# Tokens stored normed but unmodulated, scale and shift applied to transposed tokens, and one projection pass as a single fp32 product

## The chip, the cores and the metric

The kernel runs on one core of one Trainium2 chip, in fp32, as one launch. The metric is the device time of a run in microseconds; the median of three runs counts. Times in the profile are those of one further, profiled execution.

## The reference

Two transformer blocks over T = 512 tokens of width D = 1024. Each ends with a mixture of experts. What matters here is the end of the mixing, the modulated norm ahead of the router, and the experts:

```python
# block 1
mix = concat([attn, hg], -1) @ w_out
x = x + ga1 * rmsnorm(mix, ln1_post)
h = rmsnorm(x, ln2_pre) * (1.0 + sc2) + sh2
y = hierarchical_moe(h, ...)            # 32 experts, 2 per token, width 256
x = x + ga2 * rmsnorm(y, ln2_post)

# block 2
h = modulate(norm(x), shift, scale)     # h * (1 + scale) + shift
out = moe_ffn(h, ...)                   # 64 experts, 8 per token, and a shared one

def hierarchical_moe(h, ...):
    ...
    xs = tok[order // TOP_K]            # rows of h, by expert
    hg = ragged_dot(xs, w_gate, sizes)
    hu = ragged_dot(xs, w_up, sizes)
    ys = ragged_dot(silu(hg) * hu, w_down, sizes)
```

`sc2`, `sh2` (and their namesakes in block 2) are vectors over the features, the same for all tokens, from a product of the condition `c` with `w_ada`.

## The kernel before, in words

**Stages.** One program runs head, dense1 (projection in, windowed attention, a gated recurrence, projection out), the first experts, dense2, out2 (the second block's output projection, its router and its shared expert), the second experts and a last norm. Every instruction is issued through a recording helper at line 131, so every row of the profile names L131 and groups are told apart by tiles. Names: `w` and `wx` are chunks of weights (512 KB each, in two pools of buffers), `hi` and `lo` their split, `u` a 128x1024 row tile, `h` a 128x512 one, `bank` a PSUM bank, `xg` gathered token rows, `xT` their transposes, `a` and `aT` the hidden layer and its transposes, `ha_d` and `hb_d` the stored rows of the two blocks in HBM.

**Order of the work.** A cooperative scheduler (`Flow`, 152) runs generators and lets each go on when a model of the engines' times says so; the order on each engine follows from it. SP issues all weight chunks in one list, in order, as buffers come free.

**Dense products** (`steps`, 397). Each chunk of weights is split by ACT (`split_hi`, 344: a copy rounded to fp32r) and DVE (`split_lo`, 359: the rest), and `mm3` (460) adds three fp32r products, hi x lo, hi x hi and lo x hi. The left operand, the tokens, is split in the same way by `mixed` (1036). The output projection of dense1 (823 to 849) makes two passes p = 0, 1 over the 8 chunks of `w_out`, one for the token tiles 0 and 1, one for 2 and 3; each chunk gives four 128x512 products. A chunk marked `raw` is not split; the experts' chunks are of this kind, and theirs are single fp32 products.

**Post.pair** (1814) takes a pass's four banks: mean square on ACT, gate and residual on DVE, the sum to HBM (SP), the norm into two `u` tiles. `Route.tile` (1903) transposes each on PE and applies scale and shift per feature while copying out of PSUM (ACT the first four slices, DVE the last four), multiplies by the router's weights and lets DVE pick. When PE has taken the rows (`seen`), Post.pair has POOL multiply the normed rows by the scale and add the shift, both held as 128x1024 row broadcasts, and store them to `ha_d` or `hb_d` by POOL's own DMA queue. `Post.load` makes the three row broadcasts (gate, shift, scale).

**Routing.** `choose` picks the first experts after two token tiles, `finish` orders all after the fourth. `queue` (2164) lets SP load only the first experts' weights after `choose`, the rest after `finish`.

**Experts** (`run`, 2373). Per block of up to 128 tokens: a gather of rows by POOL's indirect DMA into `xg` (2218), 8 transposes on PE and two copies out of PSUM, one on ACT and one on DVE (`xT`, 2244), gate and up products over 4 chunks (`gu`, 2276), SiLU and product (`act`, 2284), transposes of `a` (2305), the down product over 2 chunks (`dn`, 2321) and a scatter-add (2330). The first stage has 32 blocks, the second 71. A block over 96 tokens makes four 128x512 products in `dn`, two per chunk.

Of the kernel before, what the change touches and what calls it, by code (L numbers as in the profile page):

```python
# [21 lines left out]
P = 128  # L22
# [191 lines left out]
class Body:  # L214
# [182 lines left out]
    def steps(self, queued, n, jobs, evac, kd=KD, pre=None, early=None):  # L397
# [6 lines left out]
        def one(c, j, sel):  # L404
            ahead = None
            for i in sel:
# [3 lines left out]
                for jj in range(c.kd):  # L410
                    s = slice(jj * n + c0, jj * n + c0 + width)
                    wt = (c.hl[0][:, s], c.hl[1][:, s])
                    ac = act(j + jj)
                    L, R = (wt, ac) if kind == "T" else (ac, wt)
                    self.mm3(outs[i], L, R, j + jj == 0, j + jj == kd - 1)
                    if jj < c.kd - 1:
                        yield
# [8 lines left out]
            self.split_lo(ahead)  # L426

# [103 lines left out]
    def ada_mask(self):  # L531

        nc = self.nc
        m = self.mask = self.c_const([P, 256])
# [34 lines left out]
    def ada_row(self, acc, b, part, dst, gain=None, plus=0.0, cols_=None):  # L569
# [11 lines left out]
        nc.sync.dma_start(cols(dst), r)  # L581
# [90 lines left out]
    def dense1(self, x1_d, h2_d, route, x1, acc1, acc2):  # L672
# [9 lines left out]
        for p in range(2):  # L682
            q_["o", p] = self.add_chunks(I["w_out"], D, KD)
        x1.queue(route)
# [28 lines left out]
        post = Post(self, True, mod[0:3], I["x"], x1_d, h2_d, route)  # L713
        route.mod = self.c_tile([P, 8]), self.c_tile([P, 8])
# [3 lines left out]
        def row(i):  # L718
            yield 8.0
            post.load(i, self.u)  # L720

        def ada(parts):
            for part in parts:
# [3 lines left out]
                if part < 5:  # L727
                    rows.append(fl.start(row(part - 2)))
# [98 lines left out]
        for p in range(2):  # L827
            fl.until_(lambda: E.done[2 * p] and E.done[2 * p + 1] and E.att[2 * p] and E.att[2 * p + 1])
            jobs = []
            for t in (2 * p, 2 * p + 1):  # L830
                act = (lambda t: lambda j: tuple(x[:, j % 4 * P : j % 4 * P + P] for x in E.half[t][j // 4]))(t)
                jobs += [("tok", half * 512, 512, act, full) for half in range(2)]
# [203 lines left out]
    def mixed(self, E, n, half, x, done):  # L1036

        hl = self.h(F32R), self.h(F32R)
# [143 lines left out]
    def dense2(self, acc_d, x2_d, route):  # L1182
# [15 lines left out]
        route.mod = self.c_tile([P, 8]), self.c_tile([P, 8])  # L1198
# [255 lines left out]
    def out2(self, mg, t_mg, x2_d, x3_d, h2_d, route, acc_d, e2):  # L1454
# [4 lines left out]
        post = Post(self, False, m[2:5], x2_d, x3_d, h2_d, route)  # L1459
        for i in range(3):  # L1460
            post.load(i, self.r4)
# [333 lines left out]
class Post:  # L1795


    def __init__(self, body, post, rows, x_d, x1_d, h2_d, route):
        self.b, self.post, self.rows, self.x_d, self.x1_d, self.h2_d = body, post, rows, x_d, x1_d, h2_d
        self.v, self.xs = [None] * 3, {}  # L1800
        self.seen, self.evac = route.seen, [False] * 2

    def load(self, i, vec):
        self.v[i] = vec()
        self.b.bcast(self.v[i], self.rows[i])
# [8 lines left out]
    def pair(self, p, outs, then):  # L1814
        b, nc = self.b, self.b.nc
        gate, shift, scale = self.v
# [24 lines left out]
        for i in range(2):  # L1841
            if i:
                nc.scalar.activation(ms[i], xs[i], AF.Copy, scale=r[:, i : i + 1])
            else:
                nc.vector.tensor_scalar(out=ms[i], in0=xs[i], scalar1=r[:, i : i + 1], scalar2=None, op0=ALU.mult)
            ts.append(b.flow.start(then(2 * p + i, ms[i]), MARGIN2))
        yield 1
        yield from b.wait_(lambda: self.seen >= {2 * p, 2 * p + 1})
        for i in range(2):
            nc.gpsimd.tensor_tensor(out=ms[i], in0=ms[i], in1=scale, op=ALU.mult)  # L1850
            nc.gpsimd.tensor_tensor(out=ms[i], in0=ms[i], in1=shift, op=ALU.add)
            nc.gpsimd.dma_start(self.h2_d[(2 * p + i) * P : (2 * p + i + 1) * P], ms[i])
# [3 lines left out]
class Route:  # L1856
# [6 lines left out]
    def __init__(self, body, E, plan, first, chosen, router, name):  # L1863
# [6 lines left out]
        self.sels, self.parts, self.chosen, self.seen = [], [None] * NT, False, set()  # L1870
# [32 lines left out]
    def tile(self, t, h, keep=None):  # L1903
# [7 lines left out]
        self.seen.add(t)  # L1911
# [245 lines left out]
class Experts:  # L2157
# [86 lines left out]
    def xT(self, x):  # L2244
        b, C = self.b, x.C
        x.xT = self.xTs[x.n % len(self.xTs)]
        for half in range(2):
# [3 lines left out]
            sl = slice(half * 4, half * 4 + 4)  # L2251
            if half:
                b.nc.vector.tensor_copy(x.xT[:, sl, :C], pt[:, :, :C])
            else:
                b.nc.scalar.activation(x.xT[:, sl, :C], pt[:, :, :C], AF.Copy)
# [227 lines left out]
def cols(w, n0, n):  # L2483

    return w[:, n0 : n0 + n].reshape(P, KD * n)
# [111 lines left out]
```

## Time and profile before

| what | value |
|---|---|
| median of 3 runs | 2090.17 us (2090.0 to 2093.3) |
| profiled execution | 2091.46 us, span 2089.7 us |
| PE, DVE, ACT, POOL busy | 87%, 51%, 27%, 17% of the span |
| HBM traffic | 495.48 MB read, 60.53 MB written, 266 GB/s over the span |
| POOL TENSOR_TENSOR of 128x1024 | 16, 40.3 us busy |
| DVE `lo`, 105 of them | 135.9 us busy |
| ACT `hi`, 105 of them | 108.8 us busy |
| ACT copies to `xT`, 103 of them | 40.0 us busy |

The time of a run lies 1.8 us above the span from the first to the last instruction. Shares are means over stages of different kinds, so they say little about any one of them: a stage is read by a window of its own. In a timeline, the number in brackets behind a row is how long its engine stood idle before it, and what released it. A weight load of PE (PEld) and its matmul (PE) are separate rows.

### The profile page before, as it was taken

How to read it: one execution, taken by the hardware profiler on the slowest of the kernel's cores; microseconds unless marked ns; L12 is line 12 of the kernel's file. 1: busy time of each engine (PE TensorE's matmuls, PEld its weight loads, DVE VectorE, ACT ScalarE, POOL GpSimd, SP SyncE). 2: the span in 40 equal slices, each digit the busy share in tenths (PEclk: the TensorE clock that was granted, in tenths of full speed). 3: DMA queues.
4: the chain of work that ended last, by engine and by line, in shares of the span. 5: the costliest groups of instructions: out<-in, count | busy, mean ns of one | idle time of the engine just before them, and what ended most of it. 6: DMA issues, size and time to landing. Idle time of an engine off the chain costs nothing. (4 is left out here: it accounts for less than half of the span.)

```text
span 2089.7 us, 35845 instructions
## 1 busy us (share of the span) xinstructions
PE 1807.8 (87%) x13085; PEld 1175.0 (56%) x13085; DVE 1061.4 (51%) x2885; ACT 559.3 (27%) x1146; POOL 359.7 (17%) x375
## 2 busy tenths in 40 slices
PE   4999986398878579888889998779999999999993
PEld 3777765354444457667767776655544445455551
DVE  5554766533223264466655655854544444444443
ACT  3522443211111252356653223410100000001011
POOL 1000002323222100000000211413222222222221
PEclk9999987599975689999999999989999999999997
DMA  9746323399999865776423557449999999999996
GB/s 338 267 153 231 141 80 140 138 347 364 376 381 380 340 221 184 259 234 173 146 84 111 181 188 265 172 152 361 362 359 358 348 363 367 353 360 346 357 357 227
DMA packets 180167, 551.81 MB, mean 264 GB/s; under 512 B 28290, under 2 KB 40706, under 8 KB 179988
## 3 DMA queue, kind: packets, MB, share of 16 engines
q1 hardware_dynamic: 159268, 491.10, 64.1%
q0 software_dynamic: 18560, 54.88, 10.6%
q10 hardware_dynamic: 2160, 3.50, 0.5%
q8 instruction: 105, 1.72, 0.3%
q14 instruction: 74, 0.61, 0.1%
HBM read 495.48 MB, written 60.53 MB: 266 GB/s over the span
## 5 line engine op out<-in xcount | busy, mean ns | idle before, releaser
L131 PE MATMUL bank<-w,xT 128*32 128x128 f32 (+5 forms) x2988 | 312.5, 363 | 12.4 <-DMA w<-in_w_gu 11.0
L131 PE MATMUL bank<-u,hi 128*128 128x512 f32 x800 | 262.9, 411 | 9.0 <-DVE u L131 5.6
L131 POOL DMA_INDIRECT acc_d<-y,iv x103 | 148.4, 1441 | 498.6 <-DVE y L131 156.9
L131 PEld LDWEIGHTS bank<-w,xT 128*32 128x32 f32 (+5 forms) x2988 | 148.7, 128 | 130.5 <-issue 70.9
L131 PE MATMUL bank<-wx,xT 128*32 128x128 f32 (+4 forms) x1812 | 185.5, 363 | 14.7 <-DMA wx<-in_w_gu 8.8
L131 DVE TENSOR_TENSOR y<-bank,gate 32x256 f32<-32x256 f32 (+5 forms) x228 | 128.0, 561 | 109.1 <-PE bank L131 107.2
L131 PEld LDWEIGHTS bank<-u,hi 128*128 128x128 f32 x800 | 148.6, 195 | 43.6 <-DVE u L131 7.1
L131 PE MATMUL bank<-u,lo 128*128 128x512 f32 x400 | 161.6, 404 | 10.2 <-DVE lo L131 10.2
L131 ACT ACTIVATE xT<-bank 128x128 f32<-128x128 f32 (+6 forms) x103 | 40.0, 388 | 450.1 <-PE bank L131 426.8
L131 DVE TENSOR_TENSOR lo<-w,hi 128x1024 fp32r<-128x1024 f32 x105 | 135.9, 1299 | 42.9 <-ACT hi L131 39.5
L131 PE MATMUL bank<-hi,u 128*128 128x512 f32 (+1 forms) x512 | 154.5, 386 | 1.4 <-DVE u L131 1.4
L131 PEld LDWEIGHTS bank<-ident,xg 48*128 48x128 f32 (+6 forms) x824 | 99.0, 200 | 75.6 <-issue 60.3
L131 PE MATMUL bank<-w,aT 128*32 128x256 f32 (+5 forms) x664 | 126.6, 535 | 14.6 <-DMA w<-in_w_dn 10.2
L131 PEld LDWEIGHTS bank<-wx,xT 128*32 128x32 f32 (+4 forms) x1812 | 89.8, 129 | 78.9 <-issue 38.7
L131 PE MATMUL bank<-wx,aT 128*32 128x256 f32 (+5 forms) x600 | 118.9, 524 | 6.6 <-DMA wx<-in_w_dn 6.0
L131 ACT ACTIVATE hi<-w 128x1024 fp32r<-128x1024 f32 x105 | 108.8, 1049 | 48.5 <-PE bank L131 24.4
L131 PE MATMUL bank<-ident,xg 48*128 48x48 f32 (+6 forms) x824 | 112.0, 280 | 11.0 <-DMA xg<-ha_d,iv 9.5
L131 PE MATMUL bank<-lo,u 128*128 128x512 f32 (+1 forms) x256 | 105.4, 412 | 17.1 <-DVE lo L131 16.1
L131 POOL TENSOR_TENSOR u<-u,t 128x1024 f32<-128x1024 f32 x16 | 40.3, 2518 | 427.3 <-DVE u L131 352.6
L131 DVE SCALAR_TENSOR_TENSOR a<-a,iv,bank 64x256 f32<-64x256 f32 (+3 forms) x80 | 38.5, 481 | 144.1 <-ACT a L131 144.1
L131 PEld LDWEIGHTS bank<-hi,u 128*128 128x128 f32 x512 | 97.6, 196 | 19.0 <-DVE u L131 1.8
L131 ACT ACTIVATE a<-bank 64x256 f32<-64x256 f32 (+4 forms) x129 | 43.4, 337 | 238.8 <-PE bank L131 230.5
(235 smaller groups left out, 2663.5 us busy)
## 6 DMA issues: line engine op xcount, KB each, us to landing
w<-in_w_gu SPq DMA_DIRECT2D x235, 512.0 KB, 13.4
wx<-in_w_gu SPq DMA_DIRECT2D x149, 512.0 KB, 12.5
w<-in_w_dn SPq DMA_DIRECT2D x101, 512.0 KB, 13.1
wa<-in_w_ada SPq DMA_DIRECT2D x96, 512.0 KB, 6.5
wx<-in_w_dn SPq DMA_DIRECT2D x91, 512.0 KB, 13.0
w<-in_w_in SPq DMA_DIRECT2D x68, 512.0 KB, 5.6
w<-in_w_out SPq DMA_DIRECT2D x21, 512.0 KB, 7.7
nab<-in_nab SPq DMA_DIRECT2D x48, 128.0 KB, 3.9
```

Source lines behind the costliest of these rows:

```text
L131: r = f(*a, **k)
```

## The change

It does three things.

1. Post.pair stores the normed rows as they are: POOL's multiplications and additions go, and so do the row broadcasts of scale and shift, the wait for `seen`, and the stores of those two vectors to HBM. The experts' `xT` applies scale and shift instead, per feature, while copying out of PSUM, as `Route.tile` does: four operations on ACT and four on DVE per block in the place of one each. The per-feature vectors are kept to the end (`c_const`); a mask becomes bf16 to make room.
2. The 8 chunks of the second pass of the first output projection are marked raw: one fp32 product in the place of three, no `hi` and `lo`; the chunk's buffer is given back after its four products.
3. `mixed` leaves the token tiles 2 and 3 of that projection unsplit.

```diff
@@ steps (397)
-                    wt = (c.hl[0][:, s], c.hl[1][:, s])
                     ac = act(j + jj)
-                    L, R = (wt, ac) if kind == "T" else (ac, wt)
-                    self.mm3(outs[i], L, R, j + jj == 0, j + jj == kd - 1)
+                    if c.raw:
+                        self.nc.tensor.matmul(outs[i], ac, c.w[:, s], start=(j + jj == 0), stop=(j + jj == kd - 1))
+                    else:
+                        wt = (c.hl[0][:, s], c.hl[1][:, s])
+                        L, R = (wt, ac) if kind == "T" else (ac, wt)
+                        self.mm3(outs[i], L, R, j + jj == 0, j + jj == kd - 1)
...
             self.split_lo(ahead)
+            if c.raw:
+                self.used(c)
@@ ada_mask (531)
-        m = self.mask = self.c_const([P, 256])
+        m = self.mask = self.c_const([P, 256], BF16)
@@ ada_row (569)
-        nc.sync.dma_start(cols(dst), r)
+        if cols_ is None:
+            nc.sync.dma_start(cols(dst), r)
@@ dense1 (672)
         for p in range(2):
             q_["o", p] = self.add_chunks(I["w_out"], D, KD)
+        for c in q_["o", 1]:
+            c.raw = True
...
-        route.mod = self.c_tile([P, 8]), self.c_tile([P, 8])
+        route.mod = self.c_const([P, 8]), self.c_const([P, 8])
...
-                act = (lambda t: lambda j: tuple(x[:, j % 4 * P : j % 4 * P + P] for x in E.half[t][j // 4]))(t)
+                cut = lambda x, j: x[:, j % 4 * P : j % 4 * P + P]
+                act = (lambda t: lambda j: cut(E.half[t][j // 4], j) if p else tuple(cut(x, j) for x in E.half[t][j // 4]))(t)
@@ mixed (1036)
+        if n >= 2:
+            E.half[n][half] = x
+            done[n] = True
+            return
         hl = self.h(F32R), self.h(F32R)
@@ out2 (1454)
-        post = Post(self, False, m[2:5], x2_d, x3_d, h2_d, route)
-        for i in range(3):
-            post.load(i, self.r4)
+        post = Post(self, False, m[2], x2_d, x3_d, h2_d, route)
+        post.load(self.r4)
@@ Post.pair (1814)
+            nc.gpsimd.dma_start(self.h2_d[(2 * p + i) * P : (2 * p + i + 1) * P], ms[i])
             ts.append(b.flow.start(then(2 * p + i, ms[i]), MARGIN2))
-        yield 1
-        yield from b.wait_(lambda: self.seen >= {2 * p, 2 * p + 1})
-        for i in range(2):
-            nc.gpsimd.tensor_tensor(out=ms[i], in0=ms[i], in1=scale, op=ALU.mult)
-            nc.gpsimd.tensor_tensor(out=ms[i], in0=ms[i], in1=shift, op=ALU.add)
-            nc.gpsimd.dma_start(self.h2_d[(2 * p + i) * P : (2 * p + i + 1) * P], ms[i])
@@ Experts.xT (2244)
-            sl = slice(half * 4, half * 4 + 4)
-            if half:
-                b.nc.vector.tensor_copy(x.xT[:, sl, :C], pt[:, :, :C])
-            else:
-                b.nc.scalar.activation(x.xT[:, sl, :C], pt[:, :, :C], AF.Copy)
+            for k in range(4):
+                j = half * 4 + k
+                if half:
+                    b.nc.vector.tensor_scalar(out=x.xT[:, j, :C], in0=pt[:, k, :C], scalar1=A[:, j : j + 1], scalar2=B[:, j : j + 1], op0=ALU.mult, op1=ALU.add)
+                else:
+                    b.nc.scalar.activation(x.xT[:, j, :C], pt[:, k, :C], AF.Identity, scale=A[:, j : j + 1], bias=B[:, j : j + 1])
```

The order of instructions moves at three places. On PE, at the beginning of the second pass of dense1's output projection (`c_467` are the router's weights, `ctx` rows of another input that are transposed in between, DMAHW and DMASW a DMA's semaphore), before:

```order
L131 MATMUL bank<-c_467,h 128x36 [waits DVE_49] x4
L131 MATMUL bank<-ident,ctx 128x128 x2
L131 MATMUL bank<-lo,h 128x512 [waits Activation_49]
L131 MATMUL bank<-hi,h 128x512
L131 MATMUL bank<-hi,h 128x512 [waits DVE_49]
L131 MATMUL bank<-lo,h 128x512
L131 MATMUL bank<-hi,h 128x512 x2
```

and now:

```order
L131 MATMUL bank<-w,h 128x512 [waits DMAHW0_49,DVE_49,PE_49]
L131 MATMUL bank<-c_467,h 128x36 [waits Activation_49] x4
L131 MATMUL bank<-c_467,h 128x36 x4
L131 MATMUL bank<-c_467,h 128x36 [waits Activation_49] x4
L131 MATMUL bank<-c_467,h 128x36 x4
L131 MATMUL bank<-ident,ctx 128x128 x2
L131 MATMUL bank<-w,h 128x512 x2
L131 MATMUL bank<-w,h 128x512 [waits PE_49]
L131 MATMUL bank<-ident,ctx 128x128 x2
L131 MATMUL bank<-w,h 128x512 [waits DMAHW1_49]
L131 MATMUL bank<-w,h 128x512 x3
```

One product of the pass now stands ahead of the router's, and the later ones wait for a chunk's DMA and not for DVE and ACT. On POOL, from the end of dense1 to the first gathers, the difference is:

```order
 L131 MEMSET u 128x1024
-L131 TENSOR_TENSOR u<-u 128x1024 x2
-L131 DMA ha_d<-u 128x1024
-L131 TENSOR_TENSOR u<-u 128x1024 x2
-L131 DMA ha_d<-u 128x1024
+L131 DMA ha_d<-u 128x1024 x2
 L131 MEMSET xg 128x1024 x3
-L131 TENSOR_TENSOR u<-u 128x1024 x2
-L131 DMA ha_d<-u 128x1024
-L131 TENSOR_TENSOR u<-u 128x1024 x2
-L131 DMA ha_d<-u 128x1024
+L131 DMA ha_d<-u 128x1024 x2
```

Only the stores are left, two per pass; out2 has the same with `hb_d`. On PE in the first experts' stage (`xT_3584`, `xT_3582` and so on are the three buffers of `xT`, in turn), one block before:

```order
L131 MATMUL bank<-ident,xg_3595 128x48 [waits DMASW4_49,PE_49]
L131 MATMUL bank<-ident,xg_3595 128x48 x7
L131 MATMUL bank<-w,xT_3584 48x256 [waits DMAHW6_49]
L131 MATMUL bank<-w,xT_3584 48x256 x3
L131 MATMUL bank<-w,xT_3584 48x256 [waits DMAHW7_49]
L131 MATMUL bank<-w,xT_3584 48x256 x3
L131 MATMUL bank<-w,xT_3582 48x256 [waits DMAHW0_49,Activation_49]
L131 MATMUL bank<-w,xT_3582 48x256 x3
```

and now:

```order
L131 MATMUL bank<-ident,xg_3469 128x48 [waits DMASW4_49]
L131 MATMUL bank<-ident,xg_3469 128x48 x7
L131 MATMUL bank<-w,xT_3458 48x256 [waits DMAHW2_49]
L131 MATMUL bank<-w,xT_3458 48x256 x3
L131 MATMUL bank<-w,xT_3458 48x256 [waits DMAHW3_49]
L131 MATMUL bank<-w,xT_3458 48x256 x3
L131 MATMUL bank<-w,xT_3456 48x256 [waits DMAHW4_49,Activation_49]
L131 MATMUL bank<-w,xT_3456 48x256
L131 MATMUL bank<-w,xT_3456 48x256 [waits Activation_49]
L131 MATMUL bank<-w,xT_3456 48x256
```

The transposes of the next block stand where they stood, two chunks of the present block ahead of their first use; what is new is a wait for ACT at each feature slice.

## Rows read from the trace of the kernel before

**Rows 1.** Experts, by stage: us, busy PE PEld DVE ACT POOL, clock, DMA, GB/s.

```profile
407.50:730.00 322.50, 256.87 (x2296) 141.01 (x2295) 95.87 (x365) 48.76 (x118) 79.04 (x73) 0.80 1.00 362
1404.00:2060.00 656.00, 639.01 (x5275) 325.78 (x5275) 302.82 (x922) 62.00 (x167) 176.44 (x206) 1.00 1.03 355
```

**Rows 2.** Waits of SP's queue, second experts' stage (1420 to 2050): total, times, longest.

```profile
SPq L131 <- DMA w<-in_w_gu: 169.5, 140, 3.5
...
SPq L131 <- PE bank L131: 16.4, 63, 0.4
```

**Rows 3.** PE timeline, 322 to 351: start, length, engine, operation, count, idle time.

```profile
322.82 3.69 PE L131 MATMUL bank<-ident,u 128*128 128x128 f32 x16 [10.85 <-DVE u L131]
...
331.87 0.47 PE L131 MATMUL bank<-lo,h 128*128 128x512 f32 x1
...
343.60 0.79 PE L131 MATMUL bank<-lo,h 128*128 128x512 f32 x1 [5.29 <-DVE lo L131]
...
346.75 0.45 PE L131 MATMUL bank<-c,c 128*128 128x32 bf16 x4
...
348.36 0.78 PE L131 MATMUL bank<-lo,h 128*128 128x512 f32 x1
...
349.56 0.40 PE L131 MATMUL bank<-lo,h 128*128 128x512 f32 x1
...
350.26 0.39 PE L131 MATMUL bank<-lo,h 128*128 128x512 f32 x1
```

**Rows 4.** The table by stage at the second pass of dense1's output projection.

```profile
301.50:328.40 26.90, 10.19 (x45) 8.99 (x45) 20.68 (x64) 10.75 (x23) 3.38 (x2) 0.50 0.29 98
349.20:367.90 18.70, 18.70 (x81) 14.64 (x80) 8.05 (x18) 2.90 (x4) 2.80 (x3) 1.00 0.69 263
```

**Rows 5.** PE weight loads, 1723 to 1727, the down product of a 128-token block.

```profile
1724.18 0.19 PEld L131 LDWEIGHTS bank<-w,aT 128*128 128x128 f32 x1 [0.24 <-issue]
1724.62 0.19 PEld L131 LDWEIGHTS bank<-w,aT 128*128 128x128 f32 x1 [0.24 <-issue]
```

**Rows 6.** DVE timeline, 306 to 316, splits ahead of the norm.

```profile
308.65 0.69 DVE L131 TENSOR_TENSOR h<-h 128x512 fp32r<-128x512 f32 x1 [0.69 <-ACT h L131]
...
312.89 0.69 DVE L131 TENSOR_TENSOR h<-h 128x512 fp32r<-128x512 f32 x1 [0.69 <-ACT h L131]
```

**Rows 7.** The page's DMA issues: count, KB each, us to landing.

```profile
w<-in_w_out SPq DMA_DIRECT2D x21, 512.0 KB, 7.7
```

**Rows 8.** POOL timeline, 384 to 396.

```profile
389.76 4.82 POOL L131 TENSOR_TENSOR u<-u 128x1024 f32<-128x1024 f32 x2
```

**Rows 9.** DVE timeline, 339 to 396, the picks of tiles 1 and 2.

```profile
339.58 0.23 DVE L131 TENSOR_SCALAR s<-c,s 128x4 f32<-128x4 f32 x1
...
339.95 0.16 DVE L131 TENSOR_SCALAR s<-s 128x4 f32<-128x4 f32 x1
...
389.91 2.24 DVE L131 TENSOR_SCALAR s<-c,s 128x4 f32<-128x4 f32 x1
...
392.30 2.31 DVE L131 TENSOR_SCALAR s<-s 128x4 f32<-128x4 f32 x1
```

**Rows 10.** DVE groups, 1307 to 1320 and 1347 to 1362 (out2): busy, mean ns.

```profile
L131 DVE TENSOR_TENSOR u<-h,u 128x512 fp32r<-128x512 f32 x4 | 8.2, 2109 | 1.3 <-ACT u L131 1.3
...
L131 DVE TENSOR_TENSOR u<-h,u 128x512 fp32r<-128x512 f32 x4 | 8.5, 2195 | 0.0
```

**Rows 11.** PE timeline in out2.

```profile
1322.65 0.79 PE L131 MATMUL bank<-lo,u 128*128 128x512 f32 x1 [7.87 <-DVE lo L131]
```

**Rows 12.** ACT groups, second experts' stage (1420 to 2050).

```profile
L131 ACT ACTIVATE xT<-bank 128x512 f32<-128x512 f32 x12 | 7.2, 597 | 66.4 <-PE bank L131 66.4
```

**Rows 13.** ACT timeline, 382 to 386, the router's tokens.

```profile
383.19 1.50 ACT L131 ACTIVATE h<-bank,c,c 128x128 f32<-128x128 f32 x4 [0.82 <-PE bank L131]
```

**Rows 14.** PE timeline, 469 to 473, between transposes and first use.

```profile
470.38 1.93 PE L131 MATMUL bank<-wx,xT 128*48 128x256 f32 x16
```

**Rows 15.** Waits of PE, second experts' stage (1420 to 2050).

```profile
PE bank L131 <- DVE a L131: 9.4, 18, 0.7
```

More of the change, by code (lines that the diff above doesn't have):

```diff
@@ L711, in dense1, with row @@
         fl.start(bounds())
-        post = Post(self, True, mod[0:3], I["x"], x1_d, h2_d, route)
-        route.mod = self.c_tile([P, 8]), self.c_tile([P, 8])
+        post = Post(self, True, mod[0], I["x"], x1_d, h2_d, route)
+        route.mod = self.c_const([P, 8]), self.c_const([P, 8])
         rows = []
-        def row(i):
+        def row():
             yield 8.0
-            post.load(i, self.u)
+            post.load(self.u)
         def ada(parts):
@@ L726, in ada @@
                 yield from self.ada_row(acc, I["b_ada"], part, mod[part - 2], *gain, cols_={3: route.mod[1], 4: route.mod[0]}.get(part))
-                if part < 5:
-                    rows.append(fl.start(row(part - 2)))
+                if part == 2:
+                    rows.append(fl.start(row()))
         def zeros():
@@ L1196, in ada @@
                                         cols_={3: route.mod[1], 4: route.mod[0]}.get(part))
-        route.mod = self.c_tile([P, 8]), self.c_tile([P, 8])
+        route.mod = self.c_const([P, 8]), self.c_const([P, 8])
         E = SimpleNamespace()
@@ L1795, with __init__, load @@
 class Post:
[L1798 to L1805, printed above, removed]
+    def __init__(self, body, post, gate, x_d, x1_d, h2_d, route):
+        self.b, self.post, self.gate, self.x_d, self.x1_d, self.h2_d = body, post, gate, x_d, x1_d, h2_d
+        self.v, self.xs = None, {}
+        self.evac = [False] * 2
+    def load(self, vec):
+        self.v = vec()
+        self.b.bcast(self.v, self.gate)
     def rows_of(self, p):
@@ L1815, in pair @@
         b, nc = self.b, self.b.nc
-        gate, shift, scale = self.v
+        gate = self.v
         xs, ms = self.xs.pop(p), [b.u() for _ in range(2)]
@@ L1869, in __init__ @@
         self.cnt, self.orow = b.c_const([P, E]), b.c_const([P, E])
-        self.sels, self.parts, self.chosen, self.seen = [], [None] * NT, False, set()
+        self.sels, self.parts, self.chosen = [], [None] * NT, False
     def setup(self):
@@ L1910, in tile @@
                 nc.tensor.transpose(pts[half][:, j * P : (j + 1) * P], h[:, half * 4 + j :: KD], b.ident)
-        self.seen.add(t)
         yield W
@@ L2244, in xT @@
     def xT(self, x):
-        b, C = self.b, x.C
+        b, C, (A, B) = self.b, x.C, self.route.mod
         x.xT = self.xTs[x.n % len(self.xTs)]
```

## The prediction

> **What bounds the kernel now.** The table by stage comes first [rows 1]: in both experts' stages the DMA share is 1.00 to 1.03 at 355 to 362 GB/s, so these 980 us last as long as their weights take to arrive; the second also keeps PE busy for 639 of 656 us, so PE has little to give there. The waits of the weight queue in the second say which of the two ends last [rows 2]: 169.5 us on transfers of one kind of chunk, 16.4 us on PE in 63 waits of at most 0.4 us, where a buffer was not free. A serial stage is different: its end lets the next stream of weights start, so whatever shortens the chain there moves all that follows. Two such stages are touched, the end of dense1 with router 1 (297 to 408 us) and out2 with router 2 (1270 to 1404 us).
>
> In the first the PE timeline [rows 3] shows where the chain stands still. The rows of token tiles 0 and 1 are transposed at 322.82 after 10.85 us of idle time for DVE; the second pass of the projection begins at 331.87, loses 5.29 us at 343.60 to a `lo` that DVE had not made, and only from 349.56 does it go on without a gap. The granted clock [rows 4] is 0.50 (1.2 GHz) between 301.5 and 328.4, where PE works in pieces, and 1.00 (2.4 GHz) from 349.2 to the end of the pass at 367.9, where it is busy without a break. The norm and the router of tiles 2 and 3 wait for that end.
>
> **Part 1, the raw second pass.** It removes 96 fp32r matmuls, 8 `hi` on ACT and 8 `lo` on DVE, and four splits of the mixed heads of tiles 2 and 3; it adds 32 fp32 matmuls.
> - *Price of PE.* A triple takes 0.70 us at 2.4 GHz (349.56 to 350.26). An fp32 product of the same shape is in the trace in the experts' down product, where a block of more than 96 tokens makes 4 of them per pair of chunks and each shows as two weight loads; those are 0.43 us apart [rows 5], so 0.86 us each. PE work thus rises from 32 x 0.70 = 22.4 to 32 x 0.86 = 27.5 us: the projection is dearer by 5.1 us and can only win by its waits. The Trainium skill, FP8 and Floating Point Precision, TensorE Precision Notes, says that a true FP32 product takes four passes through the array, which against three passes here would make it 32 x 0.93 = 29.8 us and the sum below 2.3 us worse; the row is for the very shape, so the row is taken.
> - *Start.* On DVE two mixed splits stand in the chain ahead of the norm of tiles 0 and 1, each 0.69 us after 0.69 us of waiting for ACT [rows 6]: 2.8 us go, and the transposes start at 320.0.
> - *Length.* From transposes to projection it was 322.82 to 331.87, so it starts at 329.1 now. Its only waits are for the chunks' DMAs; four raw buffers hold 4 x 3.4 us of PE work, and a chunk of w_out lands 7.7 us after its issue [rows 7], so they cover it. A raw buffer comes free only after its four products; that delays SP's later w_out loads, behind which the register loads for the experts' order stand, but the last is issued four chunks before the end and SP waits longer for the router. The counting of tokens stays in between (346.75 to 348.36, 1.6 us). 329.1 + 27.5 + 1.6 = 358.2, and 1.7 us for two products at 1.2 GHz: it ends at 359.9, where it was 367.9. **-8.0.** Best: no slow product, -9.7. Worst: 1.2 GHz throughout, 32 x 1.72 = 55 us, +18.
>
> **Part 2, the rows' scale and shift off POOL.** It removes 16 multiplications and additions of 128x1024, the row broadcasts and two small stores. The stored rows are needed only by the gathers, later than the routing, so the POOL time itself is not on the path. Its neighbours on DVE are:
> - *Router 1.* POOL works from 389.76 to 394.58 [rows 8]. The pick of tile 2 runs in it: two TENSOR_SCALAR of 128x4 take 2.24 and 2.31 us, against 0.23 and 0.16 for the same two where POOL rests, and the second ends at 394.61, POOL's pair at 394.58 [rows 9]. **-4.2.** Bounds 0 and -4.2. By the Trainium skill, SBUF — State Buffer, Who interferes with whom, a DVE instruction with one SBUF input contends only in a two-port mode, so if these two are not in one the 4.2 us would not be POOL's and the sum would be -17.2; ends 0.03 us apart speak for POOL.
> - *out2.* The `lo` parts of the shared expert's tokens, four TENSOR_TENSOR of 128x512 in each pair of tiles, take 8.2 and 8.5 us while POOL works [rows 10], against 4 x 0.69 for the same operation where POOL rests [rows 6]. 5.4 + 5.7: **-11.1.** PE stands 7.87 us behind a `lo` queued after the first four [rows 11] and ran at half clock around it, so up to 5 us more could come back; if other work of that queue is late next, half.
>
> The removed wait for `seen` and the loads of rows have neither DVE nor PE behind them: nothing.
>
> **Part 3, scale and shift in the experts.** In 103 blocks one copy on ACT and one on DVE become four operations each. The copy takes 0.60 on ACT at 128x512 [rows 12]; four per-feature operations of 128x128 on ACT take 1.50 us in the router [rows 13]. So 0.9 us more per block on ACT, and about as much on DVE. PE's order makes a block's transposes, then two chunks of the block before, then the first product on the new tokens; the trace has 1.93 us between [rows 14]. That covers 1.5 us, since the products need one feature slice at a time. Not covered are the first blocks of both stages: 0.7 each, **+1.4** (0 to 2.2). In the second stage PE waits 9.4 us for `a` of DVE [rows 15], which may be queued behind the longer xT: **+0.5** (0 to 5).
>
> **Sum.** -8.0 - 4.2 - 11.1 + 1.4 + 0.5 = -21.4 against the profiled execution's 2091.46: 2070.1. The median of the runs is 1.3 lower than that execution, so **2069 us** for the median. Both experts' stages, dense2 (its order of work is unchanged) and the end keep their lengths: they only start earlier.
>
> **Rivals.**
> - *The projection wins nothing.* PE stays at 1.2 GHz as long as it did (until 349): from 329.1 that is about 12 products at 0.86 us extra, so the second pass ends 1 us later than before. For: PE idles 10.85 us just before. Against: no wait on ACT or DVE remains to make gaps. 2069 + 9 = 2078; at 1.2 GHz throughout 2095. Chance 0.14.
> - *The DVE stretches are only half POOL's.* Other late work (MEMSETs of POOL, splits of the shared expert) takes the place, and half of 15.3 comes: 2077. Chance 0.08. That the change does nothing at all would need both.
> - *xT sets the pace of the experts, and it is slower.* PE is 97% busy in the second stage and its buffers are often full, so a delay of PE on every block delays the loads behind it. The mechanism: the first product on new tokens waits for ACT's or DVE's fourth operation, in the second stage's 71 blocks x (1.50 - 0.60) less what the smaller blocks save, some 0.75 us: 53 us, 2122 us. It decides from 21.4 / 103 = 0.21 us per block. For: [rows 1, 15]. Against: the 1.93 us of cover, and a queue that waits ten times longer on transfers than on PE. Chance 0.09.
>
> **Numbers.** Forecast 0.69, the rivals 0.14, 0.08, 0.09. A measurement of this kernel tells 0.2% (4.2 us) from no change; faster means under 2086. Of the forecast, the half-gain and most of the first rival (all but the slow clock throughout) count as faster: 0.87. Slower holds most of the xT rival and a little of the slow clock: 0.08; between, 0.05. The range reaches down to -9.7 - 4.2 - 16.1 + 0 = -30, about 2061, with 3 us for other clock gained, and up to the first two rivals together (2086): 2058 to 2085; it leaves out the xT rival and the slow clock throughout, under 0.2.
>
> **What would show it.** Right: no POOL TENSOR_TENSOR between 300 and 1362; the pick's TENSOR_SCALAR at 0.2 us; the four `lo` in out2 at 2.8 us; the second pass as 32 fp32 products without a wait for DVE, under 30 us from first to last; the first experts' gather 10 to 13 us earlier, the second stage's start 20 to 24 us earlier, both stages as long as before. Wrong: experts' stages longer with PE waiting for xT; a granted clock of 0.5 through the second pass; PE waiting elsewhere in out2 for as long as now.

## The result, and the profile after

The median of four runs is 2070.1 us (2063.66 to 2075.12), that of the kernel before beside it 2090.09 us (2089.97 to 2093.3): a ratio of 0.9887, 95% interval 0.9863 to 0.9911. A second set of runs gave 0.9878 (0.9861 to 0.9894). The profiled execution took 2071.1 us, its span 2069.3 us, 20.4 us less than before.

The first place to look is the end of dense1. The PE timeline of the changed kernel there (columns as in [rows 3]):

```profile
314.77 3.65 PE L131 MATMUL bank<-ident,u 128*128 128x128 f32 x16 [12.92 <-DVE u L131]
...
321.89 1.26 PE L131 MATMUL bank<-w,h 128*128 128x512 f32 x2 [2.33 <-issue]
322.94 6.88 PE L131 MATMUL bank<-c,h 128*128 128x36 f32 x32
...
330.09 4.15 PE L131 MATMUL bank<-w,h 128*128 128x512 f32 x6
...
343.51 17.43 PE L131 MATMUL bank<-w,h 128*128 128x512 f32 x40
373.82 3.63 PE L131 MATMUL bank<-ident,u 128*128 128x128 f32 x16 [12.88 <-DVE u L131]
377.27 3.78 PE L131 MATMUL bank<-c,h 128*128 128x36 f32 x32
```

The transposes start at 314.77 and not at 322.82. The first raw product stands ahead of the router and waits 2.33 us; the router's 16 small products (32 records, since an fp32 product shows as two) then take 6.88 us. From 330.09 on the pass has only short interruptions and ends at 343.51 + 17.43 = 360.94, where it was 367.9. One row of 40 records is 20 products, 0.87 us each: the price that was read from [rows 5]. The transposes and the router of tiles 2 and 3 were, in the kernel before:

```profile
382.06 3.65 PE L131 MATMUL bank<-ident,u 128*128 128x128 f32 x16 [14.17 <-DVE u L131]
385.51 6.88 PE L131 MATMUL bank<-c,h 128*128 128x36 f32 x32
```

They come 8.2 us earlier now, and the router takes 3.78 us and not 6.88.

On DVE, the same two instructions of tile 2's pick as the last two of [rows 9], from the DVE timeline:

```profile
380.10 0.25 DVE L131 TENSOR_SCALAR s<-c,s 128x4 f32<-128x4 f32 x1
...
380.49 0.16 DVE L131 TENSOR_SCALAR s<-s 128x4 f32<-128x4 f32 x1
```

They are at 0.25 and 0.16 us, and POOL has no TENSOR_TENSOR left in dense1 or out2. (Its others, eight of 128x1024 and eight of 128x512 in dense2, were never part of the change; the prediction's sign "none between 300 and 1362" was put too widely.) The `lo` parts of the shared expert's tokens in out2, from the groups of the stretches 1296 to 1312 and 1328 to 1342 (compare [rows 10]):

```profile
L131 DVE TENSOR_TENSOR u<-h,u 128x512 fp32r<-128x512 f32 x4 | 2.5, 686 | 0.4 <-ACT u L131 0.4
...
L131 DVE TENSOR_TENSOR u<-h,u 128x512 fp32r<-128x512 f32 x4 | 2.6, 686 | 1.9 <-DMA x_d<-u 1.9
```

2.5 and 2.6 us where it was 8.2 and 8.5. Where PE waited 7.87 us for a `lo` [rows 11], the PE timeline has one wait of 0.75 left:

```profile
1307.66 0.50 PE L131 MATMUL bank<-lo,u 128*128 128x512 f32 x1 [0.75 <-DVE lo L131]
```

In the experts the four operations show in the page's groups (mean ns after the bar), and the wait for `a` in the second stage (1407 to 2036; compare [rows 15]) has grown a little:

```profile
L131 ACT ACTIVATE xT<-bank,k,k 128x32 f32<-128x32 f32 (+6 forms) x412 | 132.9, 406 | 448.8 <-PE bank L131 395.8
...
L131 DVE TENSOR_SCALAR xT<-bank,k,k 128x32 f32<-128x32 f32 (+6 forms) x412 | 113.3, 339 | 18.5 <-PE bank L131 15.4
```

```profile
PE bank L131 <- DVE a L131: 12.0, 24, 0.6
```

The table goes by marks in the trace: the first gather of the first experts (POOL's first DMA_INDIRECT on `ha_d`), their last scatter, out2's first transposes of rows, the first gather of the second experts, their last scatter, and the span. It has all profiles but that of the plain copy of xT; the first row is the kernel before. Times in us.

| profile | first gather at | first experts | dense2 | out2 to gather | second experts | span |
|---|---|---|---|---|---|---|
| before | 409.5 | 304.4 | 592.5 | 70.6 | 687.3 | 2089.7 |
| the change | 396.1 | 302.9 | 597.7 | 57.2 | 690.4 | 2069.3 |
| the change, again | 398.2 | 301.3 | 595.5 | 57.4 | 690.7 | 2068.0 |
| projection alone | 404.2 | 303.2 | 600.5 | 70.7 | 687.8 | 2092.0 |
| rows alone | 398.8 | 303.9 | 600.9 | 58.2 | 691.8 | 2078.4 |
| POOL's work back | 400.8 | 302.6 | 596.1 | 70.0 | 691.6 | 2086.3 |
| POOL writes only | 396.9 | 304.1 | 599.7 | 59.0 | 692.8 | 2077.5 |
| half raw | 395.2 | 302.1 | 599.9 | 60.2 | 692.2 | 2074.5 |
| xT twice | 396.8 | 304.7 | 597.2 | 56.7 | 713.4 | 2093.7 |
| xT six and two | 394.7 | 305.3 | 592.1 | 58.2 | 696.2 | 2071.7 |
| both passes raw | 381.0 | 304.2 | 597.0 | 57.6 | 693.7 | 2058.3 |
| both raw, again | 379.9 | 303.5 | 597.1 | 57.6 | 691.9 | 2055.0 |
| both raw, six and two | 381.9 | 302.9 | 598.3 | 57.7 | 699.9 | 2065.2 |

Of the 20.4 us, 13.4 come up to the first gather and 13.4 in out2; dense2, whose order of work is the same, gives 5.2 back, the second experts 3.1, and the first experts and the end bring 1.9. The dense2 of the kernel before is at the short end of all thirteen (592.1 to 600.9).

Not all of the 13.4 us are the change's. Ahead of the pass PE issues the same products in the same order in both kernels. The table by stretch there (columns as in [rows 1]), before, the change and the change again:

```profile
271.00:280.00 9.00, 9.00 (x42) 8.05 (x41) 4.73 (x19) 5.41 (x9) 0.00 (x0) 0.63 0.21 60
271.00:280.00 9.00, 9.00 (x50) 7.68 (x49) 5.70 (x20) 7.13 (x11) 0.00 (x0) 0.81 0.21 59
271.00:280.00 9.00, 9.00 (x61) 7.75 (x59) 6.55 (x23) 6.93 (x11) 0.00 (x0) 1.00 0.20 59
```

The granted clock was 0.63, 0.81 and 1.00. A group of eight records of 128x64 that starts at 286.08 us before starts at 283.89 and 282.53 in the two profiles of the change; 1.6 and 3.2 us of these leads of 2.2 and 3.6 arise in the stretch. Since the clock differs between two executions of the same program, the leads are put down to chance. That leaves 11.2 us up to the first gather, and 7.7 in the second profile.

### The profile page after: what moved, and what is told of

Same layout as the page of the kernel before. It is cut to its first block, busy times and chain, and to the rows that moved or that the text cites. A ratio compares the mean times of both kernels' runs of the same rounds, so it can differ in the third digit from the quotient of the medians.

```text
span 2069.3 us, 36349 instructions
## 1 busy us (share of the span) xinstructions
PE 1805.0 (87%) x13053; PEld 1162.7 (56%) x13053; DVE 1098.4 (53%) x3182; ACT 641.6 (31%) x1443; POOL 321.4 (16%) x359
## 3 DMA queue, kind: packets, MB, share of 16 engines
q0 software_dynamic: 18560, 54.88, 10.7%
## 5 line engine op out<-in xcount | busy, mean ns | idle before, releaser
L131 ACT ACTIVATE xT<-bank,k,k 128x32 f32<-128x32 f32 (+6 forms) x412 | 132.9, 406 | 448.8 <-PE bank L131 395.8
L131 PE MATMUL bank<-u,lo 128*128 128x512 f32 x400 | 161.9, 405 | 11.3 <-DVE lo L131 11.2
L131 DVE TENSOR_TENSOR lo<-w,hi 128x1024 fp32r<-128x1024 f32 x97 | 126.3, 1307 | 38.3 <-ACT hi L131 37.5
L131 DVE TENSOR_SCALAR xT<-bank,k,k 128x32 f32<-128x32 f32 (+6 forms) x412 | 113.3, 339 | 18.5 <-PE bank L131 15.4
L131 ACT ACTIVATE hi<-w 128x1024 fp32r<-128x1024 f32 x97 | 100.7, 1049 | 35.7 <-PE bank L131 16.9
L131 POOL DMA_INDIRECT xg<-hb_d,iv x71 | 71.0, 1000 | 163.3 <-PE bank L131 69.1
L131 PEld LDWEIGHTS bank<-u,lo 128*128 128x128 f32 x400 | 78.0, 195 | 32.0 <-DVE lo L131 14.7
```

Of the source, the lines that this page charges most:

```text
L131: r = f(*a, **k)
```

## Experiments

In the later sets the kernel before had medians of 2094 to 2097 us, so ratios are compared, and marks of the table.

**The projection alone.** The kernel before with parts 2 and 3 of the diff (raw second pass, unsplit tokens) and nothing else:

```diff
         for p in range(2):
             q_["o", p] = self.add_chunks(I["w_out"], D, KD)
+        for c in q_["o", 1]:
+            c.raw = True
...
```

> The kernel before with the second pass of the output projection raw, and nothing else changed (rows still modulated by POOL). Theory: the pass is worth its 8.0 us and POOL's stretches stay, so 2082 us, with the second pass without waits for lo or hi and the first gather of the first experts' stage some 8 us earlier than before. Rival, the projection wins nothing because the fp32 product is dearer by 5.1 us: 2090 us and the first gather where it was.

Measured: 2092.1 us against 2094.3, ratio 0.9991 (0.9972 to 1.0010): no change that can be told. The mark shows what the whole time hides: the first gather comes 5.3 us earlier (1.2 of them a lead from ahead of the pass), and dense2 is 8 us longer in this profile. PE timeline:

```profile
315.72 3.65 PE L131 MATMUL bank<-ident,u 128*128 128x128 f32 x16 [12.90 <-DVE u L131]
...
323.57 1.98 PE L131 MATMUL bank<-w,h 128*128 128x512 f32 x2 [3.06 <-issue]
325.34 6.88 PE L131 MATMUL bank<-c,h 128*128 128x36 f32 x32
...
376.79 3.65 PE L131 MATMUL bank<-ident,u 128*128 128x128 f32 x16 [13.44 <-DVE u L131]
```

The transposes start 7.1 us earlier, but then PE waits 3.06 us and runs the router at 6.88 us; the second transposes come 5.3 us earlier. So in this profile the pass wins about 4 us without the rows, half of the 8 expected.

**The rows alone.** The change without its raw pass:

```diff
-        for c in q_["o", 1]:
-            c.raw = True
```

(and `mixed` and the tokens' view as before).

> The change without the raw pass: rows stored unmodulated, scale and shift in xT. Theory: 4.2 us in the first router and 11.1 in out2 come, 1.9 us of xT go, so 2077 us (13.4 less than before); the picks' TENSOR_SCALAR at 0.2 us and the four lo of out2 at 2.8 us. Rival, the stretches are half POOL's: 2084 us. Rival, xT is the pace of the experts: 2090 us or more, with experts' stages longer by more than 10 us.

Measured: 2078.8 us, ratio 0.9925 (0.9899 to 0.9951), 15.5 us less than before where 13.4 were expected. Out2 is 12.4 us shorter, the second experts 4.5 longer, and the first gather comes 10.7 us earlier (2.0 of them a lead from ahead of the pass), not 4.2. The `lo` wait inside the second pass is still there, from the PE timeline:

```profile
320.86 3.68 PE L131 MATMUL bank<-ident,u 128*128 128x128 f32 x16 [10.85 <-DVE u L131]
...
338.06 0.50 PE L131 MATMUL bank<-lo,h 128*128 128x512 f32 x1 [4.36 <-DVE lo L131]
...
374.28 3.65 PE L131 MATMUL bank<-ident,u 128*128 128x128 f32 x16 [12.88 <-DVE u L131]
```

4.36 us at 338.06 where it was 5.29 [rows 3], but from transposes to transposes the stage takes 53.4 us and not 59.2: POOL had stretched DVE in the second pass as well, under the first pick and the splits. The second step of a token split in the DVE timeline, before (POOL works from 330.68 to 335.85) and here:

```profile
331.31 2.31 DVE L131 TENSOR_TENSOR h<-h 128x512 fp32r<-128x512 f32 x1 [0.70 <-ACT h L131]
```

```profile
328.60 0.69 DVE L131 TENSOR_TENSOR h<-h 128x512 fp32r<-128x512 f32 x1 [0.70 <-ACT h L131]
```

**POOL's work back.** The change, with POOL multiplying by ones and adding zeros ahead of the store:

```diff
...
+            nc.gpsimd.tensor_tensor(out=ms[i], in0=ms[i], in1=self.one, op=ALU.mult)
+            nc.gpsimd.tensor_tensor(out=ms[i], in0=ms[i], in1=self.zero, op=ALU.add)
             nc.gpsimd.dma_start(self.h2_d[...], ms[i])
```

> The change with POOL's 16 instructions of 128x1024 put back where they stood, now multiplying by a tile of ones and adding a tile of zeros, so that the rows stay unmodulated and the rest of the change is kept. Theory: DVE stretches return (0.2 to over 1.4 us for the picks' TENSOR_SCALAR, 2.8 to over 8 us for the four lo of out2) and with them 15.3 us, so 2085 us. Rival, half: 2078 us. If POOL has no part in it: 2070 us.

Measured: ratio 0.9991 (0.9972 to 1.0010): the whole gain of the change is gone, where some 15 us of it were expected to go. In the profile the span is 17 to 18 us longer than the change's: out2 is back at 70.0 us and the first gather 2.6 to 4.7 later than in the change. DVE groups in out2, then the DVE and POOL timelines at the second router:

```profile
L131 DVE TENSOR_TENSOR u<-h,u 128x512 fp32r<-128x512 f32 x4 | 9.2, 2357 | 0.0
...
L131 DVE TENSOR_TENSOR u<-h,u 128x512 fp32r<-128x512 f32 x4 | 9.1, 2323 | 0.0
```

```profile
380.91 0.15 DVE L131 CAST s<-s 128x1 f32<-128x1 uint32 x1
...
382.63 2.16 DVE L131 CAST s<-s 128x2 f32<-128x2 uint32 x1
...
385.09 2.21 DVE L131 TENSOR_TENSOR h<-h 128x32 f32<-128x32 f32 x1
```

```profile
382.41 4.84 POOL L131 TENSOR_TENSOR u<-u 128x1024 f32<-128x1024 f32 x2
```

The stretch has moved with the timing: it is now a CAST of 128x2 and a TENSOR_TENSOR of 128x32 that take 2.16 and 2.21 us; both fall into POOL's pair, and the second ends with it (387.30 and 387.25). Which instruction pays depends on where it stands, but also on its kind: the CAST of 128x1 at 380.91 stands in POOL's first pair (376.73 to 381.51) and takes its usual 0.15 us, and the eight TENSOR_SCALARs of 128x128 beside that pair, which read PSUM, take 0.40 us each as in the change. Out2's share (12.8 us) is shown to be POOL's. The edit also restores the wait for `seen` and adds two MEMSETs of DVE; the next run has both too, so they are not the cause.

**POOL writes only.** As the run before, with five MEMSETs of a 128x1024 tile per row tile instead of the two instructions:

```diff
...
+            for _ in range(5):
+                nc.gpsimd.memset(self.one, 1.0)
```

> As the run with POOL's work put back, but POOL's instructions are five MEMSETs of 128x1024 for each row tile (0.95 us each, about as long as the two they stand for), which write SBUF and read nothing. If the stretches come from two engines reading SBUF at once, DVE runs as in the change (0.2 us for the picks' TENSOR_SCALAR, 2.8 us for the four lo) and the time is 2070 us; if any work of POOL will do, 2085 us.

Measured: 2079.7 us, ratio 0.9923 (0.9894 to 0.9951). The profile is on the first theory's side. POOL timeline and DVE groups in out2:

```profile
1301.62 5.01 POOL L131 MEMSET t<- 128x1024 f32 x5
...
1307.12 5.01 POOL L131 MEMSET t<- 128x1024 f32 x5
```

```profile
L131 DVE TENSOR_TENSOR u<-h,u 128x512 fp32r<-128x512 f32 x4 | 2.5, 687 | 0.2 <-ACT u L131 0.2
```

POOL is busy for 5 us and again 5 us, and the four `lo` take 2.5 us; the first gather and out2 are within 2 us of the change. So it is POOL's reading, not its being busy, that stretches these four. The picks were not tested: the MEMSETs of tiles 2 and 3 in dense1 end at 378.72, before the picks begin at 380.00. And for an instruction with one SBUF input the theory fails in this same profile. Two TENSOR_SCALARs of 128x64 in out2, the first under the MEMSETs (its end, 1311.17, is that of one of them, 1311.12), the second after them:

```profile
1310.35 0.82 DVE L131 TENSOR_SCALAR h<-h,s 128x64 f32<-128x64 f32 x1
...
1314.88 0.25 DVE L131 TENSOR_SCALAR h<-h,s 128x64 f32<-128x64 f32 x1
```

The change itself has such a place, 0.90 us at 1341.89 under a MEMSET of `xg`. The median lies between the two expectations all the same; in the profile it is dense2 and the second experts that are longer, 2 to 4 us each, and why they should be is left open.

**The change again.**

> The change itself, run again for the spread of its runs and a second profile. Theory: its runs spread by some 11 us because the granted clock in dense2, where the order of work is that of before, falls to 1.2 GHz at other places in each run; so the stages up to the first experts' last scatter and out2 are equal in both profiles within 1 us, and dense2 differs by several. Rival, the spread comes from the experts' stages (their loads): dense2 is equal and the experts' stages differ.

Measured: 2069.7 us (2067.07 to 2076.41), ratio 0.9878. The theory is met in part: out2 agrees to 0.2 us and dense2 differs by 2.2, but the first gather differs by 2.1 (the last scatter, at 699.0 and 699.5 us, no longer does). The 2.1 us have a visible cause, in the PE timeline of this second profile:

```profile
373.74 3.65 PE L131 MATMUL bank<-ident,u 128*128 128x128 f32 x16 [12.86 <-DVE u L131]
377.19 6.88 PE L131 MATMUL bank<-c,h 128*128 128x36 f32 x32
```

After the same idle time (12.86 and 12.88 us) the same 16 products of the router take 6.88 us here and 3.78 in the first profile; the granted clock from 377.3 to 381.0 is 0.50 here and 0.96 there. Dense2 drifts in the same way. The table by stretch of two places where both kernels issue the same work, before and the first profile of the change:

```profile
857.00:870.00 13.00, 12.05 (x39) 8.90 (x38) 7.16 (x19) 3.11 (x8) 0.00 (x0) 0.70 0.99 358
1035.00:1043.00 8.00, 7.53 (x42) 6.14 (x41) 7.58 (x31) 4.96 (x13) 0.00 (x0) 1.00 0.36 111
```

```profile
841.00:854.00 13.00, 9.27 (x40) 6.84 (x38) 6.08 (x18) 3.11 (x8) 0.00 (x0) 1.00 0.96 340
1023.00:1033.00 10.00, 9.96 (x40) 7.80 (x40) 8.52 (x33) 5.37 (x14) 0.00 (x0) 0.69 0.28 88
```

The clock was 0.70 before and 1.00 after at the first, 1.00 and 0.69 at the second: the low stretches fall at different places in each run. Over the whole of dense2 the trace has 58.7 us at 1.2 GHz before and 70.8 and 65.0 in the two profiles of the change. An estimate from these: half of the additional time is lost, 6.0 and 3.1 us, where dense2 is 5.2 and 3.0 us longer. In other profiles the estimate fails (both raw with six and two: 57.6 us at 1.2 GHz, 598.3 us long), so the clock is not all of it, and that it makes up the whole spread of runs was not shown.

**xT as a plain copy.**

```diff
-            for k in range(4):
...
+            sl = slice(half * 4, half * 4 + 4)
+            b.nc.scalar.activation(x.xT[:, sl, :C], pt[:, :, :C], AF.Copy)
```

> The change with xT made by one copy on ACT and one on DVE again; it leaves out the scale and shift of the experts' tokens. Theory: four operations in the place of one cost 1.9 us in all, so 2068 us, with both experts' stages within 2 us of the change. Rival, they cost over 0.1 us in each block: 2060 us or less.

Measured: 2103.2 us, ratio 1.0031 (1.0019 to 1.0043), 33 us more than the change. It tells nothing of the second stage: without scale and shift in the first block, the second router sees other tokens and the second experts get other rows (the trace has 72 scatters there against 71). A cost is better doubled than left out where the data steer the work. In the first stage, whose routing is the same, 293.2 us from first transposes to last scatter against 293.8 and 292.6: nothing.

**xT twice.**

```diff
-            for k in range(4):
+            for k in (0, 1, 2, 3, 0, 1, 2, 3):
```

> The change with every per-feature operation of xT made twice, the second time over the same values, so eight on ACT and eight on DVE per block. It prices the operations by doubling them. In the runs so far the second experts' stage, from the first to the last scatter, takes 645.7 and 646.3 us with plain copies and 649.3 to 652.7 with four operations; the first stage, from the first transposes to the last scatter, 293.8 and 294.6 against 292.6 to 295.2. Theory: the second stage is paced by PE where it waits for `a`, which stands behind xT in DVE's and ACT's queue, and each four operations cost 3.5 us or more there and nothing in the first: second stage 653 us or more, first stage 292 to 296. Rival, both stages go by their transfers alone and the 3.5 us are chance: second stage 646 to 651.

Measured: 2096.2 us, ratio 1.0013 (0.9998 to 1.0029), the second experts 23 us longer than in the change, the first 2 to 3. The waits of PE and of SP's queue in the second stage (1402 to 2064), then SP's in the change (1407 to 2036):

```profile
PE bank L131 <- DVE a L131: 26.5, 29, 1.4
```

```profile
SPq L131 <- PE bank L131: 169.6, 158, 5.0
```

```profile
SPq L131 <- PE bank L131: 23.1, 80, 0.9
```

PE waits 26.5 us for `a`, and SP now waits 169.6 us for buffers that PE has not freed, where the change has 23.1: much of the loads' pace has gone over from transfers to PE. The theory holds by its marks (671.9 us from the first to the last scatter, 295.4 in the first stage). In the table the stage takes 687.3 and 687.8 us with copies, 690.4 to 693.7 in the eight profiles with four operations on each engine, and 713.4 with eight: the first four cost 3 to 6 us, the next four 20 to 23. The rival that xT sets the pace is a real mechanism, and the change stands just short of it.

**xT six and two.**

```diff
-                if half:
+                if j >= 6:
```

> The change with six of the eight features slices of xT on ACT and two on DVE, in the place of four and four. If the loss in the second experts' stage comes from DVE's queue (PE waits 12.0 us for `a` there, 9.9 us before the change), DVE is relieved of two operations and the stage comes back to 648 us or less; if ACT's SiLU behind six operations is as late, 650 us or more.

Measured: 2078.0 us, ratio 0.9931 (0.9914 to 0.9948), so slower than the change; the second experts are 5 to 6 us longer (653.6 us from the first to the last scatter, so the rival's number). Waits of PE (1406 to 2038):

```profile
PE bank L131 <- DVE oh L131: 9.3, 8, 1.4
PE bank L131 <- DVE a L131: 8.9, 18, 0.6
```

The wait for `a` falls to 8.9 us as wanted, but 9.3 us for `oh`, another tile of DVE's, come in its place, which is neither the theory nor the rival's SiLU. Why `oh` is late was not followed up.

**Half of the pass raw.**

```diff
-        for c in q_["o", 1]:
+        for c in q_["o", 1][:4]:
...
```

> The change with only the first four of the second pass's eight chunks raw (and the first half of the tokens' features of tiles 2 and 3 unsplit); the last four are three fp32r products again. Theory: PE's work in the pass falls by 16 x 0.16 = 2.6 us and the splits of the last four are made while PE works on the first four, so 2067.5 us. Rival, the splits stand in DVE's queue ahead of the router's picks and PE waits for lo again: 2072 us or more.

Measured: 2073.2 us, ratio 0.9886 (0.9872 to 0.9900), not told apart from the change; by the ratio it is neither the theory's gain nor the rival's loss. PE has no wait for `lo` in the pass (from 326 us on its only wait is the one of 12.88 us for the norm), so the rival's mechanism did not occur. The first gather comes 1 to 3 us earlier; out2, untouched, is 3 us longer in this profile.

**Both passes raw.**

```diff
-        for c in q_["o", 1]:
+        for c in q_["o", 0] + q_["o", 1]:
...
```

> The change with the first pass of the output projection raw as well. Theory: fp32 is dearer on PE by 0.16 us a product and wins only where PE waited for splits; the first pass is fed by splits made ahead and keeps PE busy, so it gets up to 5 us longer and the time is about 2073 to 2075 us. Rival, what wins is the splits' work taken off ACT and DVE, which the first pass would gain by too: 2065 us or less.

Measured: 2066.8 us, ratio 0.9869 (0.9853 to 0.9884). The theory fell: the first gather comes 15 to 17 us earlier than in the change. PE timeline and table by stretch:

```profile
305.76 5.42 PE L131 MATMUL bank<-w,h 128*128 128x512 f32 x12 [3.11 <-DVE u L131]
...
314.03 1.88 PE L131 MATMUL bank<-w,h 128*128 128x512 f32 x4
319.48 2.05 PE L131 MATMUL bank<-ident,u 128*128 128x128 f32 x16 [3.57 <-DVE u L131]
...
322.45 3.66 PE L131 MATMUL bank<-c,h 128*128 128x36 f32 x32
```

```profile
290.00:320.00 30.00, 23.32 (x72) 11.27 (x71) 18.78 (x59) 9.79 (x23) 0.28 (x1) 1.00 0.29 99
```

The transposes start at 319.48, 5 us after the change's. But the second pass is already under way: its products fill the time in which PE waited for the norm (12.92 us idle in the change), the clock stays at 1.00, the router takes 3.66 us, and from transposes to transposes the stage takes 37.1 us and not 59.1. DVE's rows show why it can be: the last copy of the second pass's tokens out of PSUM, behind which its first product stands in the change (321.89), here and in the change:

```profile
297.61 0.68 DVE L131 TENSOR_TENSOR h<-bank,c 128x512 f32<-128x512 f32 x1
```

```profile
321.10 0.68 DVE L131 TENSOR_TENSOR h<-bank,c 128x512 f32<-128x512 f32 x1
```

So PE has work in the gap that waits for nobody. Whether the tokens are early because the splits are gone from ACT and DVE, as the rival has it, or because of the order that the scheduler then chose, no run tells apart. Run again:

> The version with both passes of the output projection raw, run again for its verdict and a second profile. In its first profile the first gather of the first experts' stage came at 381.0 us, where the change has 396.1 and 398.2, though its median was only 2.9 us below the change's. If the 16 us at the gather are real they repeat here within 2 us, and the median is at 2060 us or less unless dense2 or the second experts' stage are longer by what is missing; if chance, the gather is at 390 us or later.

Measured: 2062.5 us (2056.75 to 2066.48), ratio 0.9859 (0.9842 to 0.9875); the first gather is at 379.9. The gain there is real, but the medians lie only 2 to 6 us under the change's by the ratios, whose intervals overlap. Part of the rest is in both experts' stages, 1 to 3 us longer. And the two profiles are the fastest runs of their sets: their spans are 10 to 14 us under the change's, while the medians lie 6 to 7 us above the profiled executions. Why the other runs are slower is not settled. The rival's bound, 2065 us, is met in this set and not in the first. This version has the lowest ratios of the study.

**Both, with six and two.** The edits of the two versions together.

> Both passes raw and six of eight slices of xT on ACT. Theory: the two gains add, 16 us at the first gather against the change and up to 3 us in the second experts' stage: 2052 to 2062 us. Rival, the slices on ACT delay SiLU and the second stage is no shorter: as the version with both passes raw.

Measured: 2069.9 us, ratio 0.9897 (0.9879 to 0.9914): the first gather at 381.9, the second experts 6 to 8 us longer than with both passes raw. The rival was right, and worse.

## Why the prediction was right, and where its steps were not

The forecast was 2069 us, the median 2070.1; against the profiled execution -21.4 was forecast and -20.4 came. Term by term:

- *Price of an fp32 product.* 0.86 us forecast, 0.87 measured. Right, and the trace of the experts was the better source than a count of passes. From 330.09 to 360.94 the pass takes 30.9 us, and the forecast for it was 27.5 + 1.6 + 1.7 = 30.8; but the 30.9 hold 31 of the 32 products (27.0 us) and 3.9 us of other work and slow clock, where 3.3 were forecast.
- *Start.* Wrong in size: -2.8 forecast for the transposes, -8.0 measured (-7.1 with the projection alone, -2.0 with the rows alone). Of these 2.2, 1.2 and 2.0 us are the lead from ahead of the pass, which leaves 5.9, 5.9 and nothing. The step counted two splits of the tokens. A `lo` of 1.2 us at 297.2 also went from DVE's queue just ahead of the norm, and two copies of 0.7 us out of PSUM that stood between its steps were made before it: with the 2.8 forecast, 5.4 of the 5.9.
- *Length.* Wrong the other way. "From transposes to projection" was taken over as 9.05 us; it took 15.3 us. Part is the raw product ahead of the router, which waits 2.33 us; in both profiles of the change and with the projection alone its weight load starts 0.07 or 0.08 us after DVE's copy of the tokens ends, so this is the wait for DVE. The term said that the pass waits only for DMAs, though the order showed that product with a wait for DVE as well. Part is the router at 6.88 us, where it took 4.25. The errors cancel by luck: second transposes -8.2 us (-6.0 without the lead), forecast -8.0.
- *Router 1.* -4.2 forecast; from the second transposes to the first gather it is 27.4 us before, 22.3 and 24.5 in the two profiles of the change, the difference between these being the router's clock. At equal router time POOL's share is 3.0 us (before against the second profile, both 6.88) or 3.8 (26.1 with POOL's work put back, 22.3 in the first profile, both 3.8). Right as to mechanism. But the parts are not additive: alone they bring 5.3 and 10.7 us up to the first gather, together 13.4 and 11.3; without the leads 4.1 and 8.7, together 11.2 and 7.7. The rows take POOL off the second pass too, which the prediction left out. Once they have, the raw pass wins nothing that can be seen at the second transposes: 374.3 with the rows alone, 373.8 and 373.7 in the change.
- *out2.* -11.1 forecast, with up to 5 more: -13.4 and -13.2. POOL's work put back takes 12.8 of it away. Right; the part above 11.1 is within what was held possible for PE's idle time and clock.
- *xT.* +1.4 for the first blocks and +0.5 for `a`: the first stage shows nothing, the second is 3.1 to 3.4 us longer. All eight profiles with four operations give 3 to 6 us, within the bounds of both terms together but not in the first blocks, where most was forecast. The wait for `a`, the other term, is 12.0 us after 9.4. An operation takes 0.41 us on ACT on the mean (0.38 for blocks of 32 tokens, 0.46 for 128), so four cost 1.2 us more than a copy's 0.39; the prediction's guess for a mean block was 0.75.
- *dense2 "keeps its length".* It was 5.2 us longer in this profile and 3.0 in the next. The order of work is the same and the time at 1.2 GHz accounts for about as much (6.0 and 3.1 us), so this is put down to chance; but there is one profile of the kernel before only, and across all profiles it ranges over 8.8 us, more than most terms of the sum. The total was met partly by luck: this and the larger second experts offset the lead from ahead of the pass and the larger out2.

The rival of a projection that wins nothing is right by the time for the projection by itself (ratio 0.9991). In the change it is not excluded: 0.9887 and 0.9878 against 0.9925 with the rows alone, with intervals that overlap or all but touch, and second transposes where they were with the rows alone. It did not come by the rival's mechanism, since the first transposes start earlier and PE is at 0.87 us a product from 334 us on. The half-gain rival is refuted by POOL's work put back.

Of the prediction's signs the picks, the `lo` and both first gathers (13.4 and 23.1 us earlier) came about as written. The second pass did not: its first product waits for DVE, and from first product to last it takes 39.1 us, not under 30.

## What to carry to other kernels

Price an engine's work by what it does to the engine beside it: POOL's instructions were off every chain, yet they stretched much of what DVE did at the same time, and removing them was worth most of the gain (15.5 us alone, where the projection alone gave nothing that can be told). Two edits that relieve the same queue don't add up, so run each alone before crediting it. Before crediting a lead to an edit, look whether it is there already ahead of the edit's first effect: here 2.2 us were, most of it from the clock. Dearer work that waits for nobody may be moved into a gap: with both passes raw the first gather came 16 us earlier than in the change.

## What was not expected of the hardware

The same router products, after the same 12.9 us of idle PE, took 3.78 us in one execution and 6.88 in another of the same program. DVE next to a POOL that reads was stretched down to a CAST of 128x2 (2.16 us against 0.17), but not in a CAST of 128x1 (0.15) nor in a TENSOR_SCALAR that reads PSUM. POOL's MEMSETs did nothing to the four `lo`, yet held a TENSOR_SCALAR of 128x64 for 0.82 us against 0.25. And a stage that moved 355 GB/s with PE 97% busy took 3 to 6 us from a first dose of small operations and 20 to 23 from an equal second one.
